# A scheduled two-layer hybrid kernel: token shift straight from PSUM, host-laid parameters, a third weight buffer, and other costs in the model that orders the instructions

## Chip, cores, metric

One core of a Trainium2 chip runs the whole program once per launch. The metric is device time in microseconds from the runs, lower is better; the profiled execution is one more run of the same program, and every row below comes from it.

## What is computed

One inference step of a two-layer backbone over 1280 tokens (256 context tokens, 1024 latent tokens) of width 1024, in fp32. Cut to what matters here:

```python
h = rms_norm(x, g) * (1 + scale) + shift            # scale, shift, gate from SiLU(cond) @ mod_w + mod_b
# layer 0
z = h @ w_in                                        # one projection; columns split
o_a = block_attention(q, k, v) * silu(ga)
zb = z_b + mu * (0.5 * (z_prev + z_next) - z_b)     # token shift, z_prev/z_next: the neighbouring tokens, 0 at the ends
r, k, v, wl_f, wl_b, al_f, al_b = split(zb)
o_b = group_norm(rwkv7_scan(both directions)) * silu(gb)
x = x + gate * (concat(o_a, o_b) @ w_out)
# layer 1
q, k, v, g, gl = split(h @ w_in)
o = rms_norm(gla_chunked(both directions)) * silu(g)
x = x + gate * (o @ w_out)
```

Context and latent tokens are modulated by different conditioning vectors. The shift runs inside each of the two token groups; the 1280 tokens lie side by side, so the context's last token and the latent tokens' first are not neighbours.

## The kernel before

Activations lie with channels on the 128 partitions and tokens along the row. Tokens are worked in three groups (`GROUPS`: 256, 512, 512). A projection unit is 128 output columns: `split_weights` (L679) loads 512 KB of weights into `wst` (one buffer), casts them to `whi` and subtracts to get the rest `wlo` (two buffers each in layer 0), and `project_on` (L691) multiplies three times per 128 input channels (hi by hi, hi by lo, lo by hi), 24 matmuls for each group, into one of four PSUM banks `pj`; other matmuls and transposes go to four banks `a`.

The order of all instructions on all engines is set at build time by the class `Sched`. The program is written as streams of generators; `drive` (L409) repeatedly takes, among the next 13 instructions of each live task, the one that can start first by a table of modelled durations and waits (`_instr`, `_start`), and issues it. On the chip each engine then runs its own list strictly in that order. Nearly every instruction is therefore recorded at one line, L355 (`r = f(*a, **k)` in `_issue`), and rows are told apart by tile names. Where an operation may go to several engines (`copy`: ACT or DVE; `pair`: DVE or POOL; `linear`: DVE or ACT; `pcopy`: POOL, DVE or ACT) `_best` (L271) takes the engine with the earliest modelled end plus a handicap `WORTH`. DVE and POOL in use together are modelled by `_beside` (L266): of the overlap, 0.85 is added to a DVE operation and 0.25 to a POOL one.

- **Start** (`first` L851, `params` L870, `load_params` L599, `mods`, `rows`, `norms`): SP issues every transfer. 21 small ones fetch the parameters row-wise into `prow`, which TensorE transposes to `par`; TensorE also transposes the conditioning vector `cth`. The first matmuls of the modulation (`a<-mw,sT`) stand in TensorE's list behind the transpose of `prow`.
- **Token shift** (`shifted`, L789), for 14 projection units: the product is copied from PSUM to a padded row `zpad`, `(1 - mu)` times it goes to `out` (`zr` or `lr`); when all three groups are there, the two neighbours are added (`t`, a `pair`) and `mu/2` times the sum is added to `out` by one `scalar_tensor_tensor` a group.
- **RWKV operands** (`operands`, L1006) share DVE with it: `sgta`, `kd`, `wk`, and `hi`/`lo` for the head means (`a<-hi,bones`).
- **Attention and RWKV** run together afterwards (`acc<-acc,pt` sums the softmax weights; `AR`, `UV`, `Z`, `TT` belong to the RWKV chunks).
- **GLA**, layer 1 (`inner` L1880, `outputs`, `projections` L2115): for each head and group `dec` holds a chain of pairwise sums of decays, `QQ`, `KX`, `KY` are scaled level by level, while TensorE goes on with projections; `gt` carries values to be transposed.

Of the kernel before, what the change touches and what calls it, by code (L numbers as in the profile page):

```python
# [103 lines left out]
class Sched:  # L104
# [5 lines left out]
    SLOWER = {"dve": 0.85, "pool": 0.25}  # L110
    SWITCH = 0.095
    WORTH = {"dve": 0.2, "act": 0.0, "pool": 0.0}
# [63 lines left out]
    def _instr(self, name, op, f, a, k):  # L176
# [19 lines left out]
        if name == "pe":  # L196
# [15 lines left out]
            cost += 0.0025  # L212
            size = lambda x: 32 if x <= 32 else 64 if x <= 64 else P
            late = (size(rows), size(m), lhs.start_partition() // 32, out.start_partition() // 32)
        elif name == "dve":
# [16 lines left out]
            late = not psum and n >= 128 and op in ("tensor_tensor", "scalar_tensor_tensor")  # L232
# [9 lines left out]
        elif name == "pool":  # L242
# [8 lines left out]
            late = op == "tensor_tensor" and n >= 128  # L251
# [29 lines left out]
    def _start(self, ins, spare=0.0):  # L281
# [27 lines left out]
    def _issue(self, ins, t):  # L309
# [24 lines left out]
        if name in self.port and late:  # L334
            cost += self._beside(name, t, cost)
# [5 lines left out]
        elif name in self.port:  # L341
            if late:
                self.port[name] = (t - cost, t)
        elif late:
# [140 lines left out]
def tile_hybrid_dit_step(ctx: ExitStack, tc: tile.TileContext, I, C, O):  # L485
# [113 lines left out]
    def load_params(prow):  # L599
        def prm(r0, src, n):  # L600
            D.dma_start(out=prow[r0:r0 + n, :], in_=src)

        prm(R_NG, I["norm_g"].rearrange("l (k p) -> (l k) p", p=P), 16)
        prm(R_MU, I["ev_shift_mu"][:, 0:12 * P].rearrange("o (k p) -> (o k) p", p=P), 12)
        for x in range(2):
            c0 = (12 + x) * P
            D.dma_start(out=prow[R_MU + 12:R_MU + 14, 64 * x:64 * x + 64],
                        in_=I["ev_shift_mu"][:, c0:c0 + P].rearrange("o (k p) -> (o k) p", p=64))
        for i in range(2):
            prm(R_MB + 16 * i, I["mod_b"][i:i + 1, 0:2 * DM].rearrange("l (k p) -> (l k) p", p=P), 16)  # L610
        prm(R_W0, I["rw_w0"].rearrange("o d (k p) -> (o d k) p", p=P), 8)
        prm(R_A0, I["rw_a0"].rearrange("o d (k p) -> (o d k) p", p=P), 8)
        prm(R_KK, I["rw_kk"].rearrange("o (k p) -> (o k) p", p=P), 4)
        prm(R_KA, I["rw_ka"].rearrange("o (k p) -> (o k) p", p=P), 4)
        prm(R_RK, I["rw_rk"].rearrange("o (a b) k -> (o a) (b k)", b=2), 4)
# [1792 lines left out]
```

## Time and profile before

| | us |
|---|---|
| median of 3 runs (2172.52 to 2184.47) | 2178.49 |
| profiled execution | 2185.8 |
| its span, first to last instruction | 2184.0 |
| PE busy | 2026.1 (93%) |
| DVE busy | 1462.3 (67%) |
| ACT busy | 979.0 (45%) |
| POOL busy | 556.0 (25%) |

PE is TensorE's matmuls, PEld its weight loads, DVE VectorE, ACT ScalarE, POOL GpSimd; SPq is SP's queue, which issues the DMAs. A row of instructions gives how often, the time busy, the mean of one in ns, the idle time of the engine just before them and what ended most of it. PE's busy time contains stretches at half clock (mean granted clock 0.964 of full).

### The profile page before, as it was taken

Reading aid. Unit: us, or ns where it says so; the run is one execution under the profiler, and the core shown is the slowest. Engines: PE = TensorE matmul, PEld = TensorE weight load, DVE = VectorE, ACT = ScalarE, POOL = GpSimd, SP = SyncE. Lnnn points to the kernel's source line nnn. Section 1 sums busy time; section 2 is a strip of 40 time slices with the busy share of each in tenths; the row PEclk is TensorE's granted clock in tenths of the full one; section 3 lists DMA queues with packets and bytes.
Section 4 is the critical chain, followed back from the end, with each engine's and each line's share of the span. In section 5 each row is a group of like instructions: output and inputs, shape, how many; then the busy total and the mean of one; then the engine's idle time right before and its main releaser. Section 6 shows DMA issues by size and latency. Waiting matters only on the chain. (4 is left out here: it accounts for less than half of the span.)

```text
span 2184.0 us, 38916 instructions
## 1 busy us (share of the span) xinstructions
PE 2026.1 (93%) x14878; PEld 1573.9 (72%) x14878; DVE 1462.3 (67%) x2653; ACT 979.0 (45%) x2128; POOL 556.0 (25%) x661
## 2 busy tenths in 40 slices
PE   4998979899699999999999998899999999999998
PEld 2786858687477767777777764777777777778886
DVE  3549595868778787878887777553465656564454
ACT  3336354544156555665565654342445343533111
POOL 2104131312323311223212222110252445241010
PEclk8999989999799998999999999999999999999999
DMA  8224252433912142133324115442101010105553
GB/s 275 58 63 176 82 178 86 139 133 133 266 55 66 55 137 88 48 110 100 98 70 129 30 47 150 137 128 76 39 23 51 23 51 23 51 20 160 170 184 108
DMA packets 218238, 219.59 MB, mean 101 GB/s; under 512 B 20474, under 2 KB 164324, under 8 KB 218052
## 3 DMA queue, kind: packets, MB, share of 16 engines
q1 hardware_dynamic: 218052, 217.10, 31.5%
q8 instruction: 117, 1.92, 0.4%
q14 instruction: 69, 0.57, 0.1%
HBM read 149.63 MB, written 67.39 MB: 99 GB/s over the span
## 5 line engine op out<-in xcount | busy, mean ns | idle before, releaser
L355 PE MATMUL pj<-hhi,whi 128*128 128x512 f32 (+1 forms) x672 | 244.9, 366 | 15.1 <-DVE whi L355 6.9
L355 PE MATMUL pj<-hhi,wlo 128*128 128x512 f32 (+1 forms) x672 | 243.8, 364 | 5.2 <-POOL wlo L355 3.9
L355 PE MATMUL pj<-hlo,whi 128*128 128x512 f32 (+1 forms) x672 | 243.5, 364 | 0.7 <-DVE hlo L355 0.5
L355 POOL TENSOR_TENSOR acc<-acc,pt 128x512 f32<-128x512 f32 (+1 forms) x98 | 125.4, 1290 | 311.1 <-ACT pt L355 195.6
L355 PEld LDWEIGHTS pj<-hhi,whi 128*128 128x128 f32 x672 | 131.6, 196 | 38.3 <-DVE whi L355 8.0
L355 PEld LDWEIGHTS pj<-hhi,wlo 128*128 128x128 f32 x672 | 131.4, 196 | 28.4 <-issue 4.5
L355 PEld LDWEIGHTS pj<-hlo,whi 128*128 128x128 f32 x672 | 131.4, 196 | 23.6 <-issue 2.6
L355 PE MATMUL pj<-h1hi,whi 128*128 128x512 f32 (+2 forms) x304 | 112.3, 369 | 4.0 <-DVE whi L355 4.0
L355 PE MATMUL pj<-h1lo,whi 128*128 128x512 f32 (+2 forms) x304 | 113.0, 372 | 0.0
L355 PE MATMUL pj<-h1hi,wlo 128*128 128x512 f32 (+1 forms) x296 | 109.4, 370 | 0.8 <-DVE wlo L355 0.8
L355 PE MATMUL a<-h1hi,whi 128*128 128x512 f32 (+3 forms) x296 | 110.0, 373 | 0.0
L355 PE MATMUL a<-h1lo,whi 128*128 128x512 f32 (+3 forms) x296 | 109.7, 372 | 0.0
L355 PE MATMUL a<-h1hi,wlo 128*128 128x512 f32 (+1 forms) x280 | 105.8, 378 | 0.0
L355 PE MATMUL a<-pt,VO 128*64 128x512 f32 (+1 forms) x368 | 97.8, 604 | 0.3 <-ACT pt L355 0.3
L355 POOL TENSOR_SCALAR sq<-sq 128x1 f32<-128x1 f32 x70 | 19.1, 273 | 287.2 <-ACT gt L355 128.2
L355 POOL TENSOR_TENSOR QQ<-QQ,dec 128x512 f32<-128x512 f32 (+1 forms) x55 | 58.6, 1066 | 90.5 <-PE pj L355 44.3
L355 DVE TENSOR_REDUCE mx<-pj 128x1 f32<-128x512 f32 (+1 forms) x118 | 76.2, 661 | 3.4 <-PE pj L355 3.3
L355 DVE TENSOR_TENSOR acc<-acc,pt 128x512 f32<-128x512 f32 (+1 forms) x86 | 65.8, 786 | 12.0 <-ACT pt L355 8.1
L355 ACT ACTIVATE pt<-pj 128x512 f32<-128x512 f32 (+1 forms) x104 | 59.7, 590 | 22.6 <-PE pj L355 19.8
L355 PE MATMUL a<-woh,oh 128*128 128x512 f32 (+1 forms) x168 | 64.5, 384 | 4.5 <-DVE oh L355 2.8
L355 PE MATMUL a<-woh,ol 128*128 128x512 f32 (+1 forms) x168 | 64.6, 384 | 3.1 <-DVE ol L355 3.1
L355 PEld LDWEIGHTS pj<-h1hi,whi 128*128 128x128 f32 (+1 forms) x304 | 57.4, 189 | 13.3 <-issue 5.4
(524 smaller groups left out, 5695.7 us busy)
## 6 DMA issues: line engine op xcount, KB each, us to landing
mw<-in_mod_w SPq DMA_DIRECT2D x24, 1024.0 KB
ws<-wk SPq DMA_DIRECT2D x32, 512.0 KB
wst<-in_ev_w_in SPq DMA_DIRECT2D x26, 512.0 KB
wst<-in_od_w_in SPq DMA_DIRECT2D x24, 512.0 KB
AR<-ws SPq DMA_DIRECT2D x40, 256.0 KB
BK<-ws SPq DMA_DIRECT2D x40, 256.0 KB
wst<-o SPq DMA_DIRECT2D x14, 512.0 KB
Vs<-vt SPq DMA_DIRECT2D x80, 64.0 KB
```

Source lines behind the costliest of these rows:

```text
L355: r = f(*a, **k)
```

## The change

The diff has four parts.

1. **Parameters are laid out by the host.** `laid_out` transposes and stacks the small inputs before the launch, so that `cond` and `par` arrive as one transfer each; `load_params`, `prow` and both transposes are gone, and `first` and `params` are placed otherwise among the large loads.
2. **The token shift reads PSUM.** No `zpad`, no `t`: after `linear`, two `scalar_tensor_tensor` per group add `mu/2` times the neighbour directly from the bank, shifted by one column; the column at the border of groups 1 and 2 goes through a 128x1 tile `edge`.
3. **`whi` and `wlo` have three buffers in layer 0** instead of two.
4. **The model that orders the work** has other rules: a DVE or POOL operation that finds the other one's port taken waits until it is free; more operations count as using the port; a matmul is 1.06 times as long; DVE and ACT wait 0.085 us for their own results; POOL is taken only when it ends earlier by 0.6 (DVE 0.2); three operations that were fixed to DVE may go to ACT; layer 1's projections are placed as if their operands came 1.5 us later.

```diff
-    SLOWER = {"dve": 0.85, "pool": 0.25}
+    OWN = {"dve": 0.085, "act": 0.085}
-    WORTH = {"dve": 0.2, "act": 0.0, "pool": 0.0}
+    WORTH = {"dve": 0.2, "act": 0.0, "pool": 0.6}
...
-            cost += 0.0025
+            cost = 1.06 * cost + 0.0025
...
-            late = not psum and n >= 128 and op in ("tensor_tensor", "scalar_tensor_tensor")
+            late = not psum and op != "reduce_max"
...
-            late = op == "tensor_tensor" and n >= 128
+            late = op != "memset"
...
-        return max(0.0, min(t + cost, b) - max(t, a)) * self.SLOWER[name]
+        return b - t if a <= t < b else 0.0
...
-                t = max(t, w[0] + (lag(w[1]) if w[1] != name else 0.0))
+                t = max(t, w[0] + (lag(w[1]) if w[1] != name else self.OWN.get(name, 0.0)))
...
-        slots("whi", 2, [P, NK, P], F32R)
-        slots("wlo", 2, [P, NK, P], F32R)
+        slots("whi", 3, [P, NK, P], F32R)
+        slots("wlo", 3, [P, NK, P], F32R)
...
-            z = yield from get("zpad", False)
+            edge = []
+            half = parh[:, R_MU + unit:R_MU + unit + 1]
+
+            def add(o, x):
+                V.scalar_tensor_tensor(out=o, in0=x, scalar=half, in1=o, op0=ALU.mult, op1=ALU.add)
 
             def use(g, t0, n, p):
-                o = t0 + (1 if g == 0 else 2)
-                copy(z[:, o:o + n], p)
-                linear(out[:, t0:t0 + n], p, omu[:, unit:unit + 1])
-                yield
+                o = out[:, t0:t0 + n]
+                linear(o, p, omu[:, unit:unit + 1])
+                if g == 1:
+                    edge.append((yield from get("edge", False)))
+                    V.tensor_copy(edge[0], p[:, n - 1:n])
+                add(o[:, 1:n], p[:, 0:n - 1])
+                add(o[:, 0:n - 1], p[:, 1:n])
+                if g == 2:
+
+                    add(out[:, t0 - 1:t0], p[:, 0:1])
+                    add(o[:, 0:1], edge[0])
+                    put("edge", edge[0])
...
-            for g, (t0, n) in enumerate(GROUPS):
-                o = t0 + (1 if g == 0 else 2)
-                s = yield from get("t", False)
-                pair(s[:, 0:n], z[:, o - 1:o - 1 + n], z[:, o + 1:o + 1 + n], ALU.add)
-                V.scalar_tensor_tensor(out=out[:, t0:t0 + n], in0=s[:, 0:n], scalar=parh[:, R_MU + unit:R_MU + unit + 1],
-                                       in1=out[:, t0:t0 + n], op0=ALU.mult, op1=ALU.add)
-                put("t", s)
-            put("zpad", z)
...
-                V.tensor_scalar(sg, sg, 1.0, 0.0, ALU.add, ALU.add)
+                linear(sg, sg, 1.0, 1.0)
...
-              weights(0), tiles(0), *gla, (projections(), 2, None, 0), weights(1), tiles(1))
+              weights(0), tiles(0), *gla, (projections(), 2, None, 0.0, 1.5), weights(1), tiles(1))
```

Over the whole program the lists change as follows (instructions): POOL 666 to 397, among them `acc<-acc,pt` 128x512 from 92 to 53, `UV<-Vs` from 37 to 0 and `AR<-id,el` from 27 to 12; of `QQ<-QQ,dec` POOL keeps none of its 55. DVE gets 39 of the `acc` sums, 15 of `AR` and those `QQ` products, ACT the 37 `UV` copies. Of the splits `wlo<-wst,whi`, POOL had 9 in layer 0 and 3 in layer 1, and now 4 and 7. TensorE loses its three parameter transposes and is otherwise given the same matmuls in another order.

**SP at the start of the program.** `waits DMAHWn` is the semaphore lane of the transfer eight places ahead; `mw` takes modulation weights and token rows in turn. Before:

```order
L355 DMA prow<-in_ev_kn_g 1x64 [waits DMAHW1_49]
L355 DMA prow<-in_ev_qn_g 1x64 [waits DMAHW2_49]
L355 DMA prow<-in_ev_kn_g 1x64 [waits DMAHW3_49]
L355 DMA xr_177<-in_k_bones 128x128 [waits DMAHW4_49]
L355 DMA mw_184<-in_x_prompt 128x2x1024 [waits DMAHW5_49]
L355 DMA mw_185<-in_x_sample 128x2x1024 [waits DMAHW6_49]
```

After the change:

```order
L354 DMA msel<-in_k_msel 128x2
L354 DMA par<-in_k_par 128x110
L354 DMA mw_181<-in_mod_w 128x4x512
L354 DMA ident<-in_k_ident 128x128
L354 DMA mw_182<-in_x_prompt 128x2x1024 [waits DMAHW0_49]
L354 DMA mw_183<-in_x_sample 128x2x1024 [waits DMAHW1_49]
L354 DMA mw_184<-in_x_sample 128x2x1024 [waits DMAHW2_49]
```

The first token rows were the 30th transfer, behind 19 parameter transfers and `bones`; they are now the ninth, and the lane they wait for is that of `cond`, the first transfer of all.

**DVE in layer 0, third unit with a token shift.** Before:

```order
L355 TENSOR_SCALAR zr_676<-pj_142,omu 128x512
L355 CAST whi_153<-wst_131 128x1024
L355 TENSOR_TENSOR wlo_155<-wst_131,whi_153 128x1024
L355 TENSOR_TENSOR t_162<-zpad_160 128x512
L355 SCALAR_TENSOR_TENSOR zr_676<-t_163,parh,zr_676 128x256
L355 SCALAR_TENSOR_TENSOR zr_676<-t_162,parh,zr_676 128x512
L355 TENSOR_TENSOR t_163<-zpad_160 128x512
L355 SCALAR_TENSOR_TENSOR zr_676<-t_163,parh,zr_676 128x512
```

After the change:

```order
L354 SCALAR_TENSOR_TENSOR zr_650<-pj_140,parh,zr_650 128x255 x2
L354 COPY edge_164<-pj_141 128x1
L354 SCALAR_TENSOR_TENSOR zr_650<-pj_141,parh,zr_650 128x511 x2
L354 CAST whi_154<-wst_131 128x1024
L354 TENSOR_TENSOR wlo_157<-wst_131,whi_154 128x1024
L354 SCALAR_TENSOR_TENSOR zr_650<-pj_142,parh,zr_650 128x511 x2
L354 SCALAR_TENSOR_TENSOR zr_650<-pj_142,parh,zr_650 128x1
L354 SCALAR_TENSOR_TENSOR zr_650<-edge_164,parh,zr_650 128x1
```

The sums of a group now follow that group's product instead of waiting for all three, and the weights' split stands between two groups' sums; a third `wlo` (157) is in use.

**DVE in GLA, the chain of decay sums of one head and group.** Before:

```order
L355 TENSOR_TENSOR KY_13710<-KX_13707,dec_13712 128x16x16
L355 TENSOR_TENSOR dec_13713<-QQ_0_13704 128x256
L355 TENSOR_TENSOR dec_13713<-dec_13713 128x128
L355 TENSOR_TENSOR dec_13713<-dec_13713 128x64
L355 TENSOR_TENSOR dec_13713<-dec_13713 128x32
L355 TENSOR_TENSOR dec_13713<-dec_13713 128x16
L355 TENSOR_TENSOR dec_13713<-dec_13713 128x8
L355 TENSOR_TENSOR dec_13713<-dec_13713 128x4
L355 TENSOR_TENSOR Ad_13722<-pj_140,lmask 128x128
```

After the change:

```order
L354 TENSOR_TENSOR dec_13677<-QQ_0_13668 128x256
L354 TENSOR_TENSOR dec_13677<-dec_13677 128x128
L354 TENSOR_TENSOR dec_13677<-dec_13677 128x64
L354 COPY_PREDICATED Ad_13685<-lmask,pj_140 128x256
L354 TENSOR_TENSOR QQ_1_13670<-QQ_1_13670,dec_13676 128x64x2x4
L354 TENSOR_TENSOR KX_13673<-KX_13672,dec_13676 128x8x2x16
L354 TENSOR_TENSOR KY_13674<-KX_13672,dec_13676 128x8x32
L354 TENSOR_TENSOR dec_13677<-dec_13677 128x32
L354 TENSOR_TENSOR dec_13677<-dec_13677 128x16
L354 TENSOR_TENSOR dec_13677<-dec_13677 128x8
L354 TENSOR_TENSOR dec_13677<-dec_13677 128x4
```

The chain is cut in two by one level's products of the neighbouring unit, and `KX`, `KY`, `QQ` of that level, which DVE and POOL shared, now all stand in DVE's list.

## Rows read from the trace of the kernel before

**Rows 1.** Busy time by stage: each line is a stretch (us from the span's start), its length, and for every engine us busy (instructions); then the granted clock, the DMA engines' busy share and GB/s. 50 to 560 is layer 0's projections and operands, 600 to 1300 attention with RWKV, 1550 to 2000 GLA.

```profile
0.00:50.00 50.00, 22.02 (x107) 13.00 (x107) 16.95 (x46) 19.16 (x33) 10.14 (x24) 0.86 0.82 280
50.00:560.00 510.00, 466.75 (x2321) 374.16 (x2318) 359.95 (x549) 231.62 (x396) 111.57 (x93) 0.96 0.36 122
...
600.00:1300.00 700.00, 688.31 (x7295) 511.38 (x7293) 564.28 (x1230) 405.51 (x1006) 175.78 (x191) 0.99 0.26 79
...
1550.00:2000.00 450.00, 425.03 (x3116) 345.70 (x3115) 261.75 (x475) 197.79 (x446) 182.31 (x257) 0.98 0.13 39
```

**Rows 2.** The start: the DMA engines' GB/s in 40 slices of the first 60 us (1.5 us each), PE's longest waits in 0 to 50 us (engine, tile and line, what it waited for: us in total, times, longest), and SP's issues of the first large weights and of the first token rows (start us, us).

```profile
GB/s 0 49 69 382 407 389 392 384 389 379 115 8 7 1 104 380 418 426 412 404 249 280 401 410 410 385 386 385 389 390 308 195 13 5 161 408 130 0 0 0
...
PE a L355 <- DMA prow<-in_ev_kn_g: 16.0, 1, 16.0
...
2.40 2.50 SPq L355 DMA_DIRECT2D mw<-in_mod_w  x4
...
20.46 0.43 SPq L355 DMA_DIRECT2D mw<-in_x_prompt  x1
```

**Rows 3.** What PE waited for in 50 to 560 us, in the same form.

```profile
PE a L355 <- DVE hi L355: 8.9, 5, 5.7
PE a L355 <- ACT hi L355: 7.5, 6, 2.8
PE pj L355 <- DVE whi L355: 6.9, 2, 5.1
PE pj L355 <- POOL wlo L355: 3.9, 2, 2.0
PE a L355 <- DVE lo L355: 3.1, 3, 1.6
```

**Rows 4.** In order of time around 294 us, DVE, then POOL, then PE (start us, us, instruction, and in brackets the idle time before it and what ended it), and a stretch behind it with its columns as in rows 1.

```profile
294.15 2.83 DVE L355 TENSOR_TENSOR wk<-kd,sgta 128x512 f32<-128x512 f32 x1
...
298.68 1.37 DVE L355 CAST hi<-kd 128x512 fp32r<-128x512 f32 x1
300.08 0.69 DVE L355 TENSOR_TENSOR lo<-kd,hi 128x512 fp32r<-128x512 f32 x1
...
293.91 2.52 POOL L355 TENSOR_TENSOR wlo<-wst,whi 128x1024 fp32r<-128x1024 f32 x1
...
300.10 0.80 PE L355 MATMUL a<-hi,bones 128*128 128x512 f32 x1 [5.66 <-DVE hi L355]
...
296.20:303.00 6.80, 2.90 (x11) 2.63 (x12) 6.70 (x8) 1.90 (x4) 3.52 (x4) 0.50 0.64 194
```

**Rows 5.** Layer 0's token shift and what resembles its new form, groups of instructions in 0 to 560 us (us busy, mean ns | idle before).

```profile
L355 DVE SCALAR_TENSOR_TENSOR zr<-t,parh,zr 128x512 f32<-128x512 f32 x24 | 18.7, 787 | 1.0
L355 DVE TENSOR_TENSOR t<-zpad 128x512 f32<-128x512 f32 x23 | 17.8, 776 | 0.5
L355 DVE SCALAR_TENSOR_TENSOR gt<-gt,pj 128x512 f32<-128x512 f32 x14 | 9.4, 678 | 5.1 <-ACT gt L355 5.1
L355 DVE TENSOR_SCALAR zr<-pj,omu 128x512 f32<-128x512 f32 x10 | 7.5, 749 | 36.4 <-ACT zpad L355 36.4
L355 DVE TENSOR_SCALAR omu<-par 128x14 f32<-128x14 f32 x1 | 0.2, 165 | 0.0
L355 ACT COPY zpad<-pj 128x512 f32<-128x512 f32 x25 | 14.7, 586 | 65.9 <-PE pj L355 65.7
L355 ACT ACTIVATE zr<-pj,omu 128x512 f32<-128x512 f32 x14 | 9.7, 693 | 0.0
```

**Rows 6.** DVE's waits in 50 to 560 us, form as in rows 3.

```profile
DVE zr L355 <- ACT zpad L355: 36.4, 8, 8.1
DVE whi L355 <- PE pj L355: 33.9, 12, 3.9
```

**Rows 7.** Attention with RWKV: POOL's and DVE's sums in 600 to 1300 us, and the 50 us in which DVE is busiest (columns as in rows 1).

```profile
L355 POOL TENSOR_TENSOR acc<-acc,pt 128x512 f32<-128x512 f32 x81 | 104.8, 1304 | 234.7 <-ACT pt L355 180.2 <-DVE acc L355 15.3 <-PE a L355 11.1
...
L355 DVE TENSOR_TENSOR acc<-acc,pt 128x512 f32<-128x512 f32 x62 | 46.0, 756 | 9.8 <-ACT pt L355 7.9 <-PE a L355 1.5
...
...
1050.00:1100.00 50.00, 49.50 (x542) 37.86 (x541) 44.52 (x99) 27.09 (x69) 10.29 (x12) 1.00 0.22 70
```

**Rows 8.** GLA: PE's waits in 1550 to 2000 us; one of them in order of time, DVE, POOL, PE; and the products that change engine.

```profile
PE a L355 <- ACT gt L355: 11.0, 4, 3.4
PE a L355 <- DVE QQ L355: 6.4, 6, 2.7
PE pj L355 <- ACT gt L355: 5.1, 2, 2.6
PE pj L355 <- POOL QQ L355: 2.3, 1, 2.3
...
1706.72 3.78 DVE L355 TENSOR_TENSOR dec<-dec 128x128 f32<-128x128 f32 x6
...
1706.37 2.57 POOL L355 TENSOR_TENSOR wlo<-wst,whi 128x1024 fp32r<-128x1024 f32 x1
...
1712.09 0.33 PE L355 MATMUL a<-ident,gt 128*128 128x128 f32 x1 [3.36 <-ACT gt L355]
...
L355 POOL TENSOR_TENSOR QQ<-QQ,dec 128x512 f32<-128x512 f32 (+1 forms) x55 | 58.6, 1066 | 90.5 <-PE pj L355 44.3 <-PE a L355 34.0 <-DVE Ad L355 6.3
L355 DVE TENSOR_TENSOR QQ<-QQ,dec 128x512 f32<-128x512 f32 x12 | 8.8, 733 | 2.1 <-PE a L355 1.9
```

More of the change, by code (lines that the diff above doesn't have):

```diff
@@ L334, in _issue @@
         if name in self.port and late:
-            cost += self._beside(name, t, cost)
+            wait = self._beside(name, t, cost)
+            self.port[name] = (t + wait, t + wait + cost)
+            cost += wait
         self.free[name] = t + cost
@@ L340, in _issue @@
             pass
[L341 to L344, printed above, removed]
+        elif name not in self.port and late:
             self.ring = max(self.ring, t + 0.6) + late
@@ L597, in mod_cols @@
         put("m4", m4)
[L599 to L615, printed above, removed]
-        prm(R_LNG, I["rw_ln_g"].rearrange("o (k p) -> (o k) p", p=P), 4)
-        prm(R_LNB, I["rw_ln_b"].rearrange("o (k p) -> (o k) p", p=P), 4)
-        prm(R_GB, I["gla_b"].rearrange("o d (k p) -> (o d k) p", p=P), 8)
-        prm(R_GLN, I["gla_ln_g"].rearrange("o (k p) -> (o k) p", p=P), 2)
-        for h in range(2):
-            D.dma_start(out=prow[R_QN:R_QN + 1, 64 * h:64 * h + 64], in_=I["ev_qn_g"])
-            D.dma_start(out=prow[R_KN:R_KN + 1, 64 * h:64 * h + 64], in_=I["ev_kn_g"])
     def rstd_of(sq, width):
@@ L843, in layer0 @@
             sT = xp.tile([P, NK, 32], F32, name="sT")
-            cond, prow, th_ = (xp.tile([n, P], F32, name=x) for x, n in (("cond", 16), ("prow", P), ("cth", 16)))
+            cond, th_ = (xp.tile([P, 16], F32, name=x) for x in ("cond", "cth"))
             modded = [0] * 4
@@ L847, in layer0 @@
             xts = {}
[L848 to L849 removed]
             def first():
[L852 to L855 removed]
+                D.dma_start(out=cond, in_=C["k_cond"])
                 V.memset(sT, 0.0)
@@ L868, in first, with done @@
                 sch.then(done)
+                yield from sch.until(lambda: loads[0] >= 5)
+                D.dma_start(out=sT_d, in_=sT.rearrange("p k c -> p (k c)"))
             def params():
-                yield from sch.until(lambda: mod_loads[0] >= EARLY and loads[0] >= PL)
-                load_params(prow)
+                yield from sch.until(lambda: mod_loads[0] >= 2)
+                D.dma_start(out=msel, in_=C["k_msel"])
+                D.dma_start(out=par, in_=C["k_par"])
+                V.tensor_scalar(parh, par, 0.5, 0.0, ALU.mult, ALU.add)
+                V.tensor_scalar(omu, par[:, R_MU:R_MU + 14], -1.0, 1.0, ALU.mult, ALU.add)
+                def done():
+                    modded[1] += 1
+                sch.then(done)
+                yield from sch.until(lambda: mod_loads[0] >= ML)
+                D.dma_start(out=ident, in_=C["k_ident"])
+                yield from sch.until(lambda: loads[0] >= 3)
                 b = yield from get("xr", False)
@@ L876, in params @@
                 put("xr", b)
-                p = yield from get("a")
-                PE.transpose(p[:, 0:NPAR], prow[0:NPAR, :], ident[0:NPAR, 0:NPAR])
-                V.tensor_copy(par, p[:, 0:NPAR])
-                V.tensor_scalar(parh, p[:, 0:NPAR], 0.5, 0.0, ALU.mult, ALU.add)
-                put("a", p)
-                V.tensor_scalar(omu, par[:, R_MU:R_MU + 14], -1.0, 1.0, ALU.mult, ALU.add)
-                def done():
-                    modded[1] += 1
-                sch.then(done)
             def mods(n):
@@ L2396 @@
     arrays, I, C, O = {}, {}, {}, {}
-    for group, src in ((I, {n: inputs[n] for n in _INS}), (C, host_consts())):
+    for group, src in ((I, {n: inputs[n] for n in _INS}), (C, {**host_consts(), **laid_out(inputs)})):
         for name, a in src.items():
```

41 lines of the change are left out of this document (18 added, 23 removed).

## The prediction

> **What bounds the kernel now.** I read the busy times by stage first [rows 1]. PE is busy 688.3 of 700 us in attention with RWKV, 466.8 of 510 in layer 0's projections, 425.0 of 450 in GLA, and 22.0 of the first 50. TensorE is the bound, and the change leaves its matmuls as they are (three small transposes go). So only two things can be won: PE's idle time, and the time that PE loses at half clock after standing still. The second is to be seen around 294 us [rows 4]: PE stands 5.66 us, and in the 6.8 us from 296.2 the granted clock is 0.50, the lower of its two levels (1.2 GHz). For a stage I take the granted clock of rows 1: 0.96 over 510 us is 20 us lost beside 43 us of idle time, 0.98 over 450 us is 9 beside 25, 0.99 over 700 us is 7 beside 12.
>
> Next comes what ended PE's waits. At the start it is the parameters: 16.0 us for the last small transfer into `prow` [rows 2]. In layer 0 it is the weights' split, `whi` 6.9 and `wlo` 3.9, and the head means' operands, `hi` 8.9 (DVE) and 7.5 (ACT), `lo` 3.1 [rows 3]. In GLA it is `gt`, 16.1 in two rows, and `QQ`, 8.7 in two rows [rows 8].
>
> Last I looked at why these operands were late. At 294.15 DVE begins a product of 512 columns and needs 2.83 us, while POOL runs `wlo` from 293.91 to 296.43; a two-operand DVE row of the same width takes 0.69 at 300.08, when POOL is done. The cast `hi`, for which PE then waits 5.66 us, ends only at 300.05 [rows 4]. At 1706.72 the same happens in GLA: six sums `dec` take 3.78 us, because POOL's `wlo` started 0.35 us earlier; ACT's copy of `gt` comes behind them, and PE stands 3.36 us [rows 8]. A DVE operation that starts during a POOL one waits until that one has ended. This is what the new model states, and the old one put down as a part of the overlap.
>
> **Start: minus 7 us.** The GB/s row falls from 379 to 115, 8, 7, 1, 104 and is back at 380 [rows 2]: of five slices of 1.5 us, 0.6 are used at the rate of about 390 beside them, so 6.6 us of transfer time are empty while SP works through parameter transfers. With `x_prompt` ninth instead of thirtieth, its lane is that of the tiny `cond`, and the large loads follow each other. The first large load was issued at 2.40 us behind four transfers and now stands behind one: about 1 us more. All that PE does up to 50 us rests on these bytes, so I count 7 of the 7.6. Bounds: 1 us, if only the earlier issue helps; 9 us, if the first product gains from the weights' earlier place too. The 16.0 us do not come off as a whole, because the token rows are late next.
>
> **Token shift: nothing by itself.** DVE loses 23 sums `t` of 512 columns (17.8 us), 24 products `zr<-t` (18.7) and 10 `zr<-pj,omu` (7.5) [rows 5], and with the 256-column groups and `lr`, reckoned by the same durations, about 17 more: 61 us. It gains 56 sums over 511 columns from PSUM. Their form is not in the trace. The nearest rows are `gt<-gt,pj` with 0.678 (a PSUM operand, no pointer) and `zr<-pj,omu` with 0.749 (PSUM and a pointer) [rows 5]; I take the second, since the new sum has a pointer: 41.9. The 28 sums over 255 columns are an estimate from the 0.165 of a 14-column operation and the 0.749: 0.46 each, 12.8. The 42 operations on one column come to 6.9 at 0.165. Sum 61.6, as before; with 0.678 it would be 4 less. ACT loses the copies to `zpad` (14.7 and some 5) and takes 13 more `zr<-pj,omu` of 0.693: about 11 us less. POOL loses 14 sums `t`. PE needs 24 matmuls for the next group before it wants the bank back and has four banks, so the two serial sums (1.5 us) that hold it longer are covered.
> Perfetto Trace Analysis of the Trainium skill (section Optimizing Scalar/DVE Operations) speaks against this part: it gives DVE an overhead of about 60 ns on SBUF and about 125 on PSUM. By that, 84 sums cost an estimated 5.5 us more; the trace disagrees, since 0.678 from PSUM [rows 5] stands beside 0.69 for two operands of the same width in SBUF [rows 4].
>
> **Layer 0, third buffer and fewer POOL operations: minus 20 us.** DVE itself stood 33.9 us in front of `whi` until PE gave a buffer back, and 36.4 in front of `zr` behind the `zpad` copies [rows 6], with everything else in its list queued behind. A third buffer takes up the first of these, and the second goes with `zpad`. POOL's 9 `wlo` become 4, its 14 `t` go. So the waits that this can touch are `whi` 6.9, `wlo` 3.9, DVE `hi` 8.9 and `lo` 3.1 [rows 3]: 22.8 us. I take 60 per cent of them, 13.7, because one `wst` still feeds all splits and DVE keeps its load of 360 of 510 us [rows 1]; with the same share of the lost clock, 13.7 of 43 times 20, that is 20 us. Bounds: 0, and 63 (all idle time and all lost clock).
>
> **Attention with RWKV: nothing.** 39 sums `acc` come from POOL (1.304 each) to DVE; at 0.69, the duration without POOL beside it, that is 27 us, and with 15 `AR` of half the width (0.4 each, an estimate) 33 us on an engine busy 564 of 700 us [rows 1, 7]. PE idles 11.7 us there, so there is little to win. Bounds: minus 10, plus 27 (every moved sum on PE's path).
>
> **GLA: minus 8 us.** POOL's 55 `QQ` of 1.07 become DVE's at 0.73 [rows 8], so each level's operand comes 0.3 us earlier, and the `dec` chain is cut by more urgent products. Against it, seven `wlo` instead of three run on POOL, each able to hold DVE for 2 us. I take a quarter of the 25 us of idle time and 9 of clock. Bounds: 0 and minus 34.
>
> **Sum.** 7 + 20 + 8 = 35. The profiled execution took 2185.8 us and would take 2151; it lies 7.3 above the median of the three runs, and from that, 2178.5, the prediction is **2143 us**.
>
> **The rivals.** Some 0.5% (11 us) is what a measurement can tell from no change here.
> - *Only the start is won (2171).* In layer 0 and GLA the order is new everywhere, and PE meets as many late operands as before: `wst` has one buffer, so the third `whi` never gets filled in time and that part doesn't do what it says, and the DVE that stood behind POOL now stands behind its own longer list. For it: in GLA DVE carries 262 us and gets 40 for `QQ` alone [rows 1, 8]. Against it: the 33.9 us that DVE waited for a buffer [rows 6] show that the split was ready to be made. 2178.5 minus 7 is 2171.
> - *The waits born of DVE and POOL go almost whole (2096).* 22.8 us in layer 0 with 18 of clock, and 24.8 with 9 of clock in GLA, and 8 at the start: 83 us less. For it: the long rows of DVE are POOL's doing in both examples [rows 4, 8]. Against it: a list made by a model never fits all through, and ACT's `hi`, 7.5 us, has no such cause.
> - *DVE becomes the bound in attention (2199).* The 33 us moved are 2.4 us for each 50; in the busiest 50 us DVE is at 44.5 and would be at 46.9, PE at 49.5 [rows 7]. It decides from 49.5 on, twice of what is moved; or earlier, if the moved sums stand in front of the operands `TT` and `Z` that PE waits for within a microsecond. Then all 27 us of `acc` land on PE's path, the new waits cost what layer 0 and GLA gain, and 2178.5 minus 7 plus 27 is 2199. Against it: the sums that stay on DVE drop from 0.756 to 0.69 when POOL is out of the way, which gives back 4 us.
>  The Trainium skill (Perfetto Trace Analysis, Optimizing Scalar/DVE Operations) takes this side as far as DVE is full: it would hand work from a saturated DVE to ScalarE or even GpSimd, and warns that between DVE and GpSimd this might not help. By rows 1 DVE is at 81% there, so I hold its condition as not met.
>
> **How the numbers follow.** My forecast, with its own range of 2118 to 2164 (60 to 15 us won), has 0.55. Only the start has 0.17, the full gain 0.16, DVE as the bound 0.12. Faster by over 0.5% are the forecast and the full gain, 0.71; within it is the second case, 0.17; slower is the last, 0.12. The range reaches from the full gain, 2096, to 2184, just above the second case with its start term at the lower bound and a few us lost; it leaves out the slower case and the far end of the full gain.
>
> **What would show it.** Start: no empty slices in the GB/s row, the first matmul before 12 us instead of 21. Layer 0: rows `t` and `zpad` gone, sums from `pj` at 0.75 us, PE's waits for `whi` and `wlo` under 5 us, idle time in the stage under 32 us of its then length. Attention: `acc` on DVE near 0.69, PE's idle time still about 12 us; over 25 would show the last rival. GLA: no `QQ` on POOL, PE's waits for `gt` and `QQ` under 18 us together. It is wrong if PE's idle time between 50 and 2000 us does not fall, or if it falls in one stage and comes back in another.

## The result, and the profile after

| | before | after |
|---|---|---|
| median of the runs, side by side (us) | 2180.1 (2172.52 to 2184.47, 4 runs) | 2125.56 (2118.56 to 2131.31, 4 runs) |
| ratio, 95% interval | | 0.9752 [0.9711, 0.9793] |
| profiled execution / its span | 2185.8 / 2184.0 | 2118.56 / 2116.8 |
| mean granted clock | 0.964 | 0.980 |

The changed kernel is 54.5 us faster by the medians; forecast were 35. The two profiled executions differ by 67.2 us of span, because that of before lies 5.7 above its median here (longer than each of its four runs) and that of after 7.0 below (the fastest of its four). So 12.7 us of what the two traces show between them is scatter of single executions.

The page of the changed kernel, busy times:

```profile
PE 1997.0 (94%) x14876; PEld 1556.8 (74%) x14876; DVE 1456.1 (69%) x2852; ACT 1010.9 (48%) x2196; POOL 324.2 (15%) x392
```

PE was busy 2026.1 of 2184.0 us before. So its idle time fell from 157.9 to 119.8, by 38.1 us, and its busy time by 29.1 with the same matmuls. The latter is clock: if half of PE's busy time in each stretch granted 0.50 is taken as lost, the loss was 62.5 us and is 30.1. **Span = PE's work at full clock + its idle time + the half-clock loss**; the first term is 1963.6 before and 1966.9 after (and 1962 to 1972 in every kernel below), so nearly all that any of them wins is in the other two. The loss is counted from where a trace's clock record begins, at 26.5 us before and 10.7 after; the last section comes back to this.

Busy time by stage after, columns as in [rows 1]; the stages end earlier, so the stretches are shifted.

```profile
0.00:50.00 50.00, 28.26 (x131) 16.22 (x131) 19.96 (x46) 24.95 (x39) 10.85 (x24) 0.73 0.88 301
50.00:548.00 498.00, 462.26 (x2336) 369.09 (x2335) 360.76 (x619) 235.89 (x402) 65.66 (x54) 0.98 0.42 135
590.00:1290.00 700.00, 685.70 (x7154) 504.25 (x7155) 581.00 (x1278) 424.24 (x1042) 110.16 (x103) 1.00 0.28 85
1530.00:1950.00 420.00, 407.16 (x2992) 333.30 (x2991) 252.20 (x538) 190.92 (x442) 77.89 (x134) 0.99 0.16 50
```

Idle time is 35.7 us in the second stretch (43 before), 14.3 in attention (12), 12.8 of 420 in GLA (25 of 450); the clock is higher in all three. The second stretch does not hold the same work in both: after the change layer 0's last product ends at 525.5, and the first 22 us of attention, with 12 us of waits, fall into it. From the end of layer 0's norm to that product, before, then after:

```profile
74.40:559.40 485.00, 446.52 (x2187) 360.03 (x2186) 344.61 (x520) 222.54 (x382) 108.87 (x89) 0.96 0.37 124
```
```profile
66.40:525.50 459.10, 435.84 (x2191) 352.25 (x2189) 339.28 (x575) 226.19 (x385) 54.62 (x37) 0.99 0.41 133
```

This is 38.5 us of idle time and then 23.3. PE's stands (its single idle times) of 2 us and more behind the first 50 us halved, from 24 (75.3 us) to 12 (39.4); the shorter ones together did not shrink, 46.0 to 50.1 us. The stretches at 0.50, in the whole span, went from 26 to 14; of the 24 that before has behind 75 us, 18 begin at or shortly behind a stand of 2 us or more. It was mainly long stands that went, and slow stretches went with them. Over the fourteen kernels below the two go together, though not strictly: behind 75 us after has 11 such stands and 20.6 us of loss, before 24 and 56.7, jit2 22 and 62.4, but wlo_dve 21 and 36.0.

The start, GB/s of the first 60 us in slices of 1.5 us, to be held against [rows 2]:

```profile
GB/s 0 61 328 403 401 389 389 347 385 391 410 407 407 415 346 241 317 407 412 393 388 389 396 389 388 314 228 342 335 0 0 0 0 0 5 0 180 170 0 0
```

The five empty slices are gone. SP issued the first token rows at 6.87 us instead of 20.46:

```profile
6.87 0.44 SPq L354 DMA_DIRECT2D mw<-in_x_prompt  x1
```

What PE waited for: in 0 to 50 us, then the largest in 50 to 560 us, then GLA (all there is in 1530 to 1990 us), as [rows 2, 3, 8]:

```profile
PE a L354 <- DMA mw<-in_mod_w: 9.1, 4, 6.5
...
PE a L354 <- ACT hi L354: 11.9, 7, 3.1
PE a L354 <- DMA gb<-gt: 6.8, 1, 6.8
PE pj L354 <- DVE mx L354: 5.5, 3, 2.7
PE a L354 <- DVE hi L354: 2.9, 2, 2.6
PE a L354 <- POOL lo L354: 2.7, 3, 1.1
PE a L354 <- DVE lo L354: 2.7, 3, 1.7
...
PE a L354 <- DVE QQ L354: 6.4, 5, 2.2
PE pj L354 <- DVE QQ L354: 6.4, 4, 1.9
```

`gb<-gt` and `mx` belong to attention's first products, behind 525.5. `whi` and `wlo` are no longer in the list of layer 0, nor is `gt` in GLA's. ACT's `hi` grew from 7.5 to 11.9; `QQ`, now DVE's alone, is 12.8 instead of 8.7.

DVE in layer 0 after: the new sums as groups (us busy, mean ns | idle before), and DVE's own waits, as [rows 5, 6]:

```profile
L354 DVE SCALAR_TENSOR_TENSOR zr<-pj,parh,zr 128x511 f32<-128x511 f32 x48 | 35.8, 746 | 7.0 <-ACT zr L354 6.2
L354 DVE SCALAR_TENSOR_TENSOR zr<-pj,parh,zr 128x255 f32<-128x255 f32 x24 | 11.5, 481 | 6.7 <-ACT zr L354 6.3
...
DVE edge L354 <- ACT zr L354: 22.1, 6, 4.7
...
DVE zr L354 <- ACT zr L354: 16.3, 11, 3.8
...
DVE whi L354 <- PE pj L354: 14.0, 6, 2.9
```

The durations are the ones taken from the neighbours, 0.749 and 0.46. DVE's wait for a weight buffer fell from 33.9 to 14.0. Its wait for ACT's `zpad`, 36.4, did not go: DVE now waits 22.1 + 16.3 = 38.4 for ACT's `linear` ahead of the sums.

Attention, the sums `acc` that DVE does in 590 to 1290 us (ns: least, median, most):

```profile
L354 DVE TENSOR_TENSOR acc<-acc,pt x111: 406/685/1770, 597.6 to 1289.1; 128x512 f32<-128x512 f32 x108, 128x256 f32<-128x256 f32 x3
```

### The profile page after: what moved, and what is told of

Read it like the earlier page. It is cut to its first block, busy times and chain, and to the rows that moved or that the text cites. A ratio compares the mean times of both kernels' runs of the same rounds, so it can differ in the third digit from the quotient of the medians.

```text
span 2116.8 us, 38599 instructions
## 1 busy us (share of the span) xinstructions
PE 1997.0 (94%) x14876; PEld 1556.8 (74%) x14876; DVE 1456.1 (69%) x2852; ACT 1010.9 (48%) x2196; POOL 324.2 (15%) x392
## 3 DMA queue, kind: packets, MB, share of 16 engines
q1 hardware_dynamic: 218080, 217.10, 32.6%
## 4 chain that ended last, share of the span: by engine, by line
PE 55%; DVE 11%; issue 3%; ACT 3%; DMA 2%; POOL 1%; SPq 0%; POOLq 0%; DVEq 0%; ACTq 0%
PE pj L354 28%; PE a L354 27%; DVE QQ L354 2%; DVE mx L354 1%; DVE dec L354 1%; ACT QQ L354 1%; DVE LL L354 1%; DVE gt L354 1%; DMA gb<-gt 1%; DMA x<-xt 1%; DVE acc L354 1%; DVE TT L354 1%; DVE Z L354 1%; POOL wol L354 0%; DMA wst<-o 0%
## 5 line engine op out<-in xcount | busy, mean ns | idle before, releaser
L354 PE MATMUL pj<-hhi,wlo 128*128 128x512 f32 (+1 forms) x672 | 239.4, 360 | 2.2 <-DVE wlo L354 2.2
L354 POOL TENSOR_TENSOR acc<-acc,pt 128x512 f32<-128x512 f32 (+1 forms) x57 | 75.8, 1337 | 457.1 <-ACT pt L354 325.7
L354 DVE TENSOR_TENSOR acc<-acc,pt 128x512 f32<-128x512 f32 (+1 forms) x127 | 89.0, 724 | 11.1 <-ACT pt L354 8.7
L354 DVE TENSOR_REDUCE mx<-a 128x1 f32<-128x512 f32 (+1 forms) x86 | 56.6, 669 | 14.9 <-PE a L354 14.9
L354 PE MATMUL pj<-woh,oh 128*128 128x512 f32 (+1 forms) x160 | 61.1, 382 | 5.0 <-DVE oh L354 5.0
L354 PEld LDWEIGHTS a<-h1hi,whi 128*128 128x128 f32 (+1 forms) x304 | 56.5, 186 | 11.1 <-ACT whi L354 1.9
L354 PEld LDWEIGHTS pj<-h1lo,whi 128*128 128x128 f32 (+1 forms) x296 | 56.3, 190 | 10.5 <-DVE h1lo L354 1.7
```

## The experiments

**Theory 1**: a DVE operation is held by a POOL one, and the new model keeps them apart; most of the gain beyond the start comes from the order. **Theory 2** (rival): the gain comes from parts that need no new model, the start, the third buffer and the later placing of layer 1's projections (`1.5`, which the prediction did not price). **Theory 3** (rival): a new order is a new draw, and a part of the difference is luck.

Each kernel was timed beside the kernel before. The table gives the ratio, and from one profiled execution: the end of stage A (the last transposes of layer 0's norm) and, as *idle + half-clock loss* in us, B (from there to the last `Tm,LT` product of RWKV: projections, attention, nearly all of RWKV), C (to the first `QQ,KX` product of GLA), D (the rest of GLA and the end). Each order was made once and profiled once, so a row of the table carries the draw and the execution with it.

| kernel | ratio [95%] | A ends | B | C | D |
|---|---|---|---|---|---|
| before | 1 | 74.4 | 100.8 | 33.6 | 48.0 |
| after | 0.9752 [0.9711, 0.9793] | 66.4 | 58.0 | 26.6 | 33.6 |
| start_only | 0.9939 [0.9917, 0.9960] | 64.2 | 89.0 | 35.4 | 42.2 |
| shift_only | 0.9991 [0.9972, 1.0009] | 71.8 | 91.8 | 33.9 | 42.9 |
| shift_buf3 | 0.9884 [0.9863, 0.9906] | 74.1 | 77.8 | 32.6 | 44.2 |
| buf2 | 0.9777 [0.9750, 0.9804] | 67.2 | 78.5 | 30.7 | 30.7 |
| spare_only | 0.9935 [0.9919, 0.9951] | 73.9 | 101.6 | 34.4 | 27.3 |
| m_only | 0.9836 [0.9811, 0.9862] | 71.5 | 87.9 | 24.4 | 34.8 |
| m_old | 0.9724 [0.9697, 0.9751] | 64.1 | 66.2 | 31.7 | 32.0 |
| wlo_dve | 0.9929 [0.9906, 0.9951] | 73.8 | 79.9 | 32.0 | 40.7 |
| mold_wlo | 0.9706 [0.9683, 0.9729] | 65.8 | 57.4 | 32.9 | 32.2 |
| jit1 | 0.9945 [0.9930, 0.9961] | 74.2 | 87.6 | 29.7 | 42.2 |
| jit2 | 1.0056 [1.0035, 1.0077] | 74.2 | 110.1 | 32.7 | 49.0 |
| jit3 | 0.9874 [0.9848, 0.9899] | 66.3 | 73.7 | 47.4 | 36.2 |

**start_only**: the kernel before with the parameters laid out by the host.

```diff
-            cond, prow, th_ = (xp.tile([n, P], F32, name=x) for x, n in (("cond", 16), ("prow", P), ("cth", 16)))
+            cond, th_ = (xp.tile([P, 16], F32, name=x) for x in ("cond", "cth"))
...
+                D.dma_start(out=par, in_=C["k_par"])
```

> The kernel before with the host-laid parameters and the new start alone. My term of the prediction: 7 us faster than before (2171 to 2174), bounds 1 and 9; the last product of the norms' transposes at 66 to 68 us instead of 74.4, no empty slices in the GB/s row. Rival: the 8 us at the start are given back at the next wait (weights or zpad), 0 to 2 us.

0.9939, about 13 us. The stage that it touches ends 10 us earlier; the rest of the 13 is the later order, drawn anew (B falls by 12 here, as it does in jit1 for no reason). Stage A ended at 64.2 us, earlier than the 66 to 68 expected. It is the cleanest term of all: the six kernels with the new start end it at 64.1 to 67.2 (mean 65.7), the eight others at 71.5 to 74.4 (mean 73.5), 7.8 us apart without overlap.

**shift_only** and **shift_buf3**: the token shift from PSUM in the kernel before, without and with the third pair of weight buffers; start and model are those of before.

```diff
-            z = yield from get("zpad", False)
...
+                add(o[:, 1:n], p[:, 0:n - 1])
+                add(o[:, 0:n - 1], p[:, 1:n])
```
```diff
-        slots("whi", 2, [P, NK, P], F32R)
-        slots("wlo", 2, [P, NK, P], F32R)
+        slots("whi", 3, [P, NK, P], F32R)
+        slots("wlo", 3, [P, NK, P], F32R)
```

> The kernel before with the token shift from PSUM alone (old start, two weight buffers, old model). My sum gives the shift itself nothing, and its absence of zpad waits a part of layer 0's 20: 0 to 10 us faster. If layer 0's gain is the shift's: 15 to 20 us faster. If the banks that are held longer hurt: slower by up to 10 us, with PE waiting for pj's readers.

> The kernel before with the token shift from PSUM and the third pair of weight buffers, with the start and the planner's model of before. The shift alone ran at 0.9991, and the changed kernel loses 6 us when the third pair is taken away. If the third buffer is worth something of its own in layer 0: about 2165 to 2172 us (0.993 to 0.996), with the stage of the layer-0 projections under 478 us where the kernel before needs 484.6, and the waits of PE on whi and wlo nearly gone. If the buffer only pays under the new model (one wst feeds every split, and the old list doesn't place the split earlier): 2173 to 2180 us, ratio 0.996 to 1.000, and a stage of 482 to 485 us.

The shift alone is no change, 0.9991. With the third pair the kernel takes 2155.75 us; 0.9991 to 0.9884 is 23 us, more than either expectation, and about twice what a new draw of this kernel moves (jit1 and jit2, below). Layer 0's projections, from the first product behind stage A to the last, took 484.6 us before and with the shift 484.4; with the third pair they take 463.4. PE's waits for the weights' split in 50 to 560 us, shift_only:

```profile
PE pj L355 <- POOL wlo L355: 5.8, 3, 2.0
...
PE pj L355 <- ACT whi L355: 4.9, 3, 2.8
...
PE pj L355 <- DVE wlo L355: 1.0, 1, 1.0
```

and shift_buf3, PE's one such wait and DVE's for a buffer:

```profile
PE pj L355 <- DVE wlo L355: 3.6, 3, 1.9
...
DVE whi L355 <- PE pj L355: 17.1, 7, 2.9
```

11.7 us of PE's waits became 3.6 under the old model. DVE's wait for a buffer, 33.9 before, is 25.4 with the shift alone and 17.1 with the third pair. The one `wst` that feeds all splits does not stop the third buffer from paying. That this is not the draw is to be seen over all fourteen kernels: from the end of stage A to the end of layer 0's projections, without the last two token groups of the last unit (jit3 puts these behind attention's first stands), the five with three pairs take 448 to 453 us, the nine with two 457 to 479.

**buf2**: the changed kernel with two pairs.

```diff
-        slots("whi", 3, [P, NK, P], F32R)
-        slots("wlo", 3, [P, NK, P], F32R)
+        slots("whi", 2, [P, NK, P], F32R)
+        slots("wlo", 2, [P, NK, P], F32R)
```

> The changed kernel with two whi and wlo buffers in layer 0 instead of three. If the third buffer is what took PE's waits for whi and wlo and DVE's 33.9 us in front of whi: 8 to 15 us slower than the changed kernel, and DVE waits in front of whi for PE again for 20 us or more. If one wst buffer bounds the splits anyway, or DVE had time to stand there: within 4 us.

0.9777 against 0.9752: some 5 us, less than the 8 to 15 expected, and the intervals overlap. In the trace B loses 20 us more than after (this execution lies 6 us above its median, that of after 7 below), the layer's projections take 474.0 us against 458.6, PE waits 8.0 us for `whi` and `wlo` again, and DVE 25.7 in front of `whi`. The place answers as expected; the time of the whole kernel answers less. Its order is another draw, which may be why.

**spare_only**: the kernel before with only the projections of layer 1 placed later.

```diff
-              weights(0), tiles(0), *gla, (projections(), 2, None, 0), weights(1), tiles(1))
+              weights(0), tiles(0), *gla, (projections(), 2, None, 0.0, 1.5), weights(1), tiles(1))
```

> The kernel before with layer 1's projections placed as if their operands came 1.5 us later, alone. I gave this nothing. The changed kernel with the old model is as fast as with the new one, and its stretch from the first to the last GLA product is 374 us instead of 404; if that is this line's: 10 to 20 us faster than before, PE's waits for gt (16.1 us) gone, layers before it untouched. If the GLA gain comes from what the order does by chance: within 4 us.

0.9935, 14 us. PE's list is that of before up to 1466 us, and A, B and C agree with before within 1 us; D falls from 48.0 to 27.3. PE's waits for `QQ` and `gt` in 1550 to 2000 us, spare_only:

```profile
PE a L355 <- DVE QQ L355: 4.1, 3, 2.7
...
PE a L355 <- POOL QQ L355: 2.9, 1, 2.9
PE pj L355 <- DVE gt L355: 1.2, 1, 1.2
PE pj L355 <- ACT gt L355: 1.0, 2, 0.8
```

The 16.1 us for `gt` [rows 8] are 2.2, though POOL keeps its `QQ` and the model is the old one. By the edit the transposes of `gt`, which belong to the projections, are put into PE's list as if `gt` came 1.5 us later, so that other products stand in front of them. Over the table, the six kernels with `1.5` have D at 27.3 to 36.2 (mean 32.0), the seven others without it and without the new model 40.7 to 49.0 (mean 44.2).

**m_only** and **m_old**: the new model in the kernel before, and the changed kernel with the old model.

```diff
-    SLOWER = {"dve": 0.85, "pool": 0.25}
+    OWN = {"dve": 0.085, "act": 0.085}
...
-        return max(0.0, min(t + cost, b) - max(t, a)) * self.SLOWER[name]
+        return b - t if a <= t < b else 0.0
```

(and the other lines of the model; m_old takes them all back. The `1.5` and the three operations that may go to ACT are not in m_only, and stay in m_old.)

> The kernel before with the new ordering model alone (port, own waits, longer products, POOL only when it ends 0.6 us earlier); start, token shift and two weight buffers as before. Theory 1 (the model is the larger part, because DVE is held less by POOL): 20 to 35 us faster than before, ratio 0.984 to 0.991, the gain in layer 0, attention and GLA, none in the first 75 us; DVE's time in the six dec sums and in wk<-zr,E falls to its duration without POOL. Theory 2 (the gain is that of the code: start, shift, buffers): 0 to 8 us, ratio 0.996 to 1.000. Theory 3 (any new order is a draw): either sign, up to 10 us.

> The changed kernel with the old ordering model; new start, shift from PSUM, three weight buffers, and the projections' later placing in layer 1 stay. Theory 1: 20 to 35 us slower than the changed kernel (2145 to 2160), POOL has again some 80 acc sums and nearly 60 QQ products. Theory 2: 8 us slower at most (2125 to 2134). The start's gain, 7 to 9 us up to the first 75 us, is there by both.

m_only lies at the far edge of theory 1's range, m_old near theory 2's (2122.45 us; 2125 to 2134 expected). On the old code the model is worth 1.6 per cent, 36 us, the largest single part, in one draw. One of its signs failed: the products `wk<-zr,E` of 512 columns, which were to fall to their duration without POOL, take 887 ns in the mean instead of 858 (919 in after). On top of the other parts nothing of it is to be seen: 0.9724 without it, 0.9752 with it, and over all kernels that have the other parts 0.9706 and 0.9724 (mold_wlo, m_old) against 0.9752 and 0.9874 (after, jit3). The stages suggest why: alone it brings D to 34.8, where `1.5` brings it too, and B to 87.9, where the third buffer does more and where jit1, a mere draw, stands as well. So the parts seem to take the same waits; a run that shows one wait taken by either was not made. Without the model the parts measured alone (0.61 + 1.16 + 0.65 per cent) add up to 2.42, and m_old has 2.76 [2.49, 3.03]; the model's 1.64 on top of that would give 4.1, and after has 2.48. Each of these numbers carries a draw of some 0.6 per cent. **Theory 1 falls** for the combination.

**wlo_dve**: the kernel before, its order kept word for word; the 14 remainders `wlo` and `wol` that POOL computes are issued by DVE at their place.

```diff
+        if name == "pool" and any(x.startswith(("wlo", "wol")) for x in writes):
+            f = self.nc.vector.tensor_tensor
```

> The kernel before with its order kept word for word, except that the 14 subtractions wlo and wol that stood in POOL's list are issued by DVE at the same place of the program. If a POOL operation that holds DVE is what makes the operands late: DVE's 1.23 us each replace up to 2.6, the six dec sums at the two places fall from 3.8 to under 2.5 us, PE's two waits of 3.36 us and the one of 5.66 us shrink, 8 to 15 us faster than before in all. If DVE's list is the bound whoever holds it: 14 times 1.23 more on DVE, 0 to 10 us slower.

0.9929: giving an engine at 67 per cent 14 operations more makes the kernel 15 us faster. The place around 294 us [rows 4], DVE and PE, in wlo_dve:

```profile
293.86 1.75 DVE L357 TENSOR_TENSOR wk<-kd,sgta 128x512 f32<-128x512 f32 x1
...
297.31 0.43 DVE L357 CAST hi<-kd 128x512 fp32r<-128x512 f32 x1
297.77 0.69 DVE L357 TENSOR_TENSOR lo<-kd,hi 128x512 fp32r<-128x512 f32 x1
298.38 1.22 DVE L357 TENSOR_TENSOR wlo<-wst,whi 128x1024 fp32r<-128x1024 f32 x1
...
297.79 0.79 PE L357 MATMUL a<-hi,bones 128*128 128x512 f32 x1 [3.63 <-DVE hi L357]
```

`hi` takes 0.43 instead of 1.37, `wk` 1.75 instead of 2.83 (other POOL products still run beside it), and PE stands 3.63 instead of 5.66. The split that took POOL 2.52 takes DVE 1.22. At 1706 [rows 8] PE no longer stands for `gt`. This shows the mechanism with no new order beside it. That the split itself comes sooner is not what pays in layer 0: PE's waits for `whi` and `wlo` there are 13.5 us in before and 13.2 in wlo_dve. The Trainium skill says why (SBUF — State Buffer, section Who interferes with whom): a DVE operation with two SBUF inputs and a GpSimd one that reads SBUF share a port pair, and who issues first holds it; the trace agrees for `wk`, whose row shrinks where POOL's is taken away, while `hi`, which shrinks too, is a cast with one input, which this rule on two inputs does not cover.

**mold_wlo**: m_old with the same two lines, a try to beat both kernels.

> The changed kernel with the planner's model of before (2122.45 us in its run) and the weights' remainders that it gives to POOL issued by DVE at the same place of the order. If the waits of DVE behind a POOL product are what the new model saves, they are saved here without it: 2105 to 2115 us (0.966 to 0.972), the time DVE spends above the short durations of its groups falls from 152 us to about 120, and GLA's end gains most. If those waits lie beside PE's work in this order (its GLA stage is already the shortest, with 7.2 us of idle time): 2118 to 2127 us, 0.971 to 0.976.

2117.67 us, 0.9706, between the two expectations. It is the fastest kernel here, but its interval overlaps that of m_old (0.9724), so a further gain is not shown. DVE's time above the lower quartile of each group of its instructions (same operation, tiles and shape), summed, falls from 127 us (m_old) to 109; in after it is 88, in before 151. (The 152 and 120 of the expectation were reckoned in another way.) After has the fewest of these stalls of the four and is not the fastest, so most of them seem to lie beside PE's work.

**jit1, jit2, jit3**: a new draw of the order by a number that means nothing; jit1 and jit2 from the kernel before, jit3 from the changed one.

```diff
-    SWITCH = 0.095
+    SWITCH = 0.1
```
```diff
-            cost += 0.0025
+            cost += 0.003
```

(the first in jit1 and jit3, the second, TensorE's cost, in jit2)

> The kernel before with one number of the model changed that has no meaning for any of the theories: the modelled cost of switching the TensorE array's size 0.100 instead of 0.095 us. The order differs from 300 us on. If a new order is a draw of some size, this shows the size: I expect within 10 us of before, either sign. If it is 20 us faster, what the other kernels won by a new order says little on their causes.

> The kernel before with one number of the planner's model changed that means nothing here: each TensorE operation is reckoned 0.5 ns longer (0.0025 to 0.003 us). It measures how far the time moves when the order is drawn anew for no reason. The other such draw, SWITCH from 0.095 to 0.100, gave 0.9945. If the kernel before is a middling draw: 2172 to 2188 us (0.996 to 1.004). If it is an unlucky draw, so that every other order gains: 2158 to 2172 us (0.991 to 0.996), and then some 10 us of what each part of the change gave is only the new draw.

> The changed kernel with SWITCH at 0.100 in place of 0.095, which again means nothing. If draws scatter by some 0.5 per cent around a middle and the changed kernel is a middling one: 2115 to 2136 us (0.970 to 0.980 of the kernel before). If it is a lucky draw: 2136 to 2150 us (0.980 to 0.987), and a part of its 54 us belongs to the draw.

The three draws of before have 0.9945, 1 and 1.0056: a middling draw, with 12 us to either side. jit2's 2195.1 lies above both expectations. So does the changed kernel's second draw, jit3: 2152.46 us, 27 over the first. Of the 35 us between the two profiled spans 21 lie in C and 16 in B. The 21 have one place, at the end of attention in jit3 (PE's rows, the DMA that it waits for, DVE's work on `wst`):

```profile
1310.81 0.38 PE L354 MATMUL a<-acc,ones 128*64 128x256 f32 x1
1339.49 0.55 PE L354 MATMUL pj<-woh,oh 128*128 128x256 f32 x1 [28.29 <-DVE oh L354]
...
1334.14 0.60 SPq L354 DMA_DIRECT2D wst<-o  x1
...
1332.88 1.23 DVE L354 TENSOR_TENSOR wol<-wst,woh 128x1024 fp32r<-128x1024 f32 x1
1338.65 0.69 DVE L354 CAST oh<-wst 128x1024 fp32r<-128x1024 f32 x1 [4.54 <-DMA wst<-o]
```

Attention's products are all done at 1311, and the first `o` to be read back is issued only at 1334, when DVE is done with weights that were loaded into the same `wst`. In after the first `wst<-o` is issued at 1304, while attention still has products, and the same wait is 6.33 us. **Theory 3 holds in part**: an order is worth about 0.6 per cent either way in before, and 1.2 between the two draws of after. The change itself is far outside of it: its draws have 0.9752 and 0.9874, its near relatives 0.9706 to 0.9777, and those of before 0.9945 to 1.0056.

## Why the prediction was right, and where it was not

- **Start, 7 us: right, in size too.** 7.8 us by the ends of stage A. The first product starts at 6.5 us.
- **Token shift, nothing: right** (0.9991), by the forecast durations. The Trainium skill's larger DVE overhead on PSUM (Perfetto Trace Analysis, section Optimizing Scalar/DVE Operations), which spoke for 5.5 us more, is not to be seen: the new sums of 511 columns take 746 ns from PSUM, and those of 512 that they replace took a median of 750 from SBUF (787 in the mean [rows 5], as some ran beside POOL).
- **Layer 0, third buffer, 20 us: the mechanism right, the split between its two terms not.** The third pair gave 23 us in shift_buf3, takes `whi` off PE's list there and both off it in after. To the layer's last product, idle time fell by 15.2 us (13.7 forecast) and the half-clock loss by 11.4 (6). The sign "idle time under 32" failed at 35.7 in the stretch that was named, because attention's first stands are in it. Wrong was also "the second goes with `zpad`": the wait came back as one for ACT's `zr`.
- **The clock: the mis-sized term.** I let it fall in proportion to idle time, where I saw any won: 6 us in layer 0 and 2 in GLA, beside some 27 of idle time at start, layer 0 and GLA. Measured by the pair of traces were 38 of idle time and 32 of clock. In terms of idle time and clock, attention and RWKV gave 3.1 and 13.0, where I had nothing; C, for which I had no term, 1.8 and 5.2; D 9.4 and 5.0, where I had 6 and 2. The stands that went were mostly the long ones, and it is with those that the rows show 0.50. One such place of before is in attention: PE stands from 812.64 to 816.39, and from 815 on it has 17 us at 0.50. In after the same products come at 781, without a stand. In spare_only, which gives PE the same list up to there, the same stand took 1.47 us and the clock stayed at 1.00. (Before, then spare_only: the row and the stretch; then after's stretch; columns as in [rows 1].)

```profile
816.38 0.47 PE L355 MATMUL pj<-id,sm 64*64 64x64 f32 x2 [3.75 <-ACT ring L355]
...
815.00:832.00 17.00, 15.62 (x110) 12.73 (x111) 8.95 (x21) 6.82 (x21) 0.00 (x0) 0.50 0.20 65
```
```profile
823.60 0.33 PE L355 MATMUL pj<-id,sm 64*64 64x64 f32 x2 [1.47 <-ACT ring L355]
...
822.00:839.00 17.00, 15.50 (x187) 12.16 (x184) 15.94 (x35) 9.78 (x28) 0.94 (x2) 1.00 0.47 129
```
```profile
780.00:797.00 17.00, 17.00 (x191) 13.79 (x189) 13.89 (x32) 12.25 (x32) 3.29 (x3) 1.00 0.56 185
```

  So a part of the clock that before lost is the luck of one execution. Behind stage A the three draws of before lose 41 to 62 us, the two of after 22 and 34: some 25 of the 32 us outlast the draw.
- **Attention, nothing: idle time right, clock not.** Idle time 12 to 14 us, but 0.99 to 1.00 of 700 us is some 7 us. **DVE as the bound** did not come: 581 of 700 us busy, `acc` at a median of 0.685.
- **GLA, 8 us: about the size, the wrong cause.** It gave 12 (means of D), and that much comes with the later placing of the projections alone, which the prediction left without a price. `QQ` on DVE, to which it gave the gain, is not needed for it (m_old and spare_only keep `QQ` on POOL), and PE waits longer for `QQ` than before. That the time came near the forecast here is luck.
- **The waits of DVE and POOL as the core: wrong for the combination.** The mechanism is real (wlo_dve), and a part of the 20 us of layer 0 and much of GLA's 8 were built on it. But with the third buffer and the later projections the new model adds nothing that these runs can tell from a draw.
- **Sum, 35 against 54.5.** By the traces of the pair, which differ by 67, the clock (24 us over the forecast) is the largest part of what is missing, and idle time 11; 12.7 of this is the scatter of the two executions. And the draw of the order moves the sum by as much: jit3, the same change in another draw, has 27 us less of it. How much of the 54.5 is this draw stays open, with two draws of after.

## What to carry to other kernels

Ask of each stand of the bounding engine how long it is: one long stand mostly cost its length and a slow stretch behind it here, so ending it was worth more than its share of idle time, while the short stands came back elsewhere. Price every edit, a number in a priority too: the `1.5` that looked like nothing is enough for GLA's whole gain. And before giving a gain to a scheduler's new rules, draw the order anew with a number that means nothing: here that alone moves the kernel before by 12 us to either side and the changed one by 27, and the gains of the parts do not add.

## What the runs showed of the hardware

**POOL is held too.** In the changed kernel DVE runs two-operand work without a gap from 1294.94 to 1302.10, at its short durations; POOL's one `wol` beside it takes 9.19 us and ends 2.24 us behind DVE's last, where POOL's `wlo` of the same size take 2.45 in the mean. This is one place of one trace. The load of `o` into the same `wst` and PE's wait hang on it (POOL, DVE, SP, PE):

```profile
1295.15 9.19 POOL L354 TENSOR_TENSOR wol<-wst,woh 128x1024 fp32r<-128x1024 f32 x1 [7.17 <-DVE woh L354]
...
1294.94 2.48 DVE L354 TENSOR_TENSOR acc<-acc,pt 128x512 f32<-128x512 f32 x4
1297.35 1.21 DVE L354 TENSOR_TENSOR wol<-xt,woh 128x1024 fp32r<-128x1024 f32 x1
1298.48 2.49 DVE L354 TENSOR_TENSOR acc<-acc,pt 128x512 f32<-128x512 f32 x4
1300.89 1.21 DVE L354 TENSOR_TENSOR wol<-xt,woh 128x1024 fp32r<-128x1024 f32 x1
...
1304.37 0.60 SPq L354 DMA_DIRECT2D wst<-o  x1
...
1309.62 0.58 PE L354 MATMUL a<-woh,oh 128*128 128x256 f32 x1 [6.33 <-DVE oh L354]
```

**A granted clock of 1.00 in a row is not always measured.** From 14.2 to 34.5 us the row of after says 0.50 and that of jit3, below, says 1.00, at the same 380 GB/s, and their norm stages end at 66.4 and 66.3, as if half clock cost nothing there. But the clock record of jit3's trace begins only at 34.4 us. PE's products of 256 columns start 0.21 us apart in jit3 in that stretch, as they do in after at 0.50, and 0.12 apart at 54.72, where jit3's record does say 1.00:

```profile
14.20:34.50 20.30, 12.39 (x53) 9.60 (x54) 7.71 (x17) 12.57 (x22) 7.20 (x14) 1.00 1.07 380
...
30.91 0.41 PE L354 MATMUL pj<-hlo,whi 128*128 128x256 f32 x1
31.12 0.41 PE L354 MATMUL pj<-hhi,wlo 128*128 128x256 f32 x1
...
54.72 0.28 PE L354 MATMUL pj<-hlo,whi 128*128 128x256 f32 x1
54.84 0.28 PE L354 MATMUL pj<-hhi,wlo 128*128 128x256 f32 x1
```

So both ran at half clock, and what it cost there no run here tells. It also explains PE's work at full clock: start_only, m_old, buf2 and jit3, whose records begin at 34 to 36 us, are the four kernels that seemed to need 1970 to 1972 us of it. With half clock reckoned for what lies before the record, all fourteen need 1961 to 1965.
